# One 512 KB load cut into five copies, so that 9 of the 16 DMA engines carry more of it: linear ReLU attention on one Trainium2 core

## The chip, the core and the metric

The kernel runs on one core of a Trainium2 chip. The metric is the device time of one execution in microseconds (us), as the median of several runs. The profile comes from one more execution of the same program.

The core has five engines that matter here: TensorE (PE, matrix products), VectorE (DVE), ScalarE (ACT), GpSimd (POOL) and SyncE (SP). Data is moved between memory (HBM) and the core's own memory (SBUF) by 16 DMA engines that all copies share. A copy is issued by an engine's queue. In this kernel POOL issues most copies (the profile's queue q0) and SP issues the first four loads and the last three stores (queue q1). Each DMA engine serves both queues.

## What is computed

Q, K and V are float32, of shape batch 8, heads 12, sequence 512, depth 64. For each of the 96 heads:

```python
Q_feat = np.maximum(0, Q)
K_feat = np.maximum(0, K)
KV = np.einsum('bhkd,bhkv->bhdv', K_feat, V)
K_sum = np.sum(K_feat, axis=2)
numerator = np.einsum('bhqd,bhdv->bhqv', Q_feat, KV)
denominator = np.einsum('bhqd,bhd->bhq', Q_feat, K_sum)
return numerator / (denominator[:, :, :, None] + 1e-10)
```

## The kernel before, in words

The 96 heads are handled in 12 blocks `o` of 8 heads. A block has two groups `g = 2*o` and `g = 2*o + 1` of 4 heads each. In SBUF a group of K or V is a tile of 128 rows (partitions) of 16 x 64 = 1024 numbers, and a block of Q or of the output is 128 rows of 2048 numbers. In memory each row is one contiguous stretch: 4096 bytes for a group's row, 8192 bytes for a Q or output row.

**Loads.** The first two groups (block 0) are loaded as float32 by SP, in the loop of lines 111 to 115: K of group 0, V of group 0, K of group 1, V of group 1, each one copy of 128 x 4096 bytes into a tile `kv_first`. These tiles come from the pool `outp`, which later holds the output tiles `o_sb`. All other loads are issued by POOL and turned into bfloat16 on the way: `load_q(0)`, then `load(1)` to `load(5)`, each being K, V and Q of a block. From then on the order of POOL's queue is written out in `store` (line 262): the store of block `o`, then `load(o + 6)`. POOL's copies use eight semaphores in turn, so the ninth copy waits until the first has landed: at most eight are under way. The last two blocks are stored by SP (lines 267 and 270), the last one in two halves.

**Compute.** The order is written out by hand (`manual_schedule`), each engine running its instructions in program order. For a group, `prep` (line 144) has DVE build `kf` from K (line 147) and one half of `vo` from V (line 149), and `prep_v` (line 152) builds the other half of `vo`, on ACT (line 154) or DVE (line 156). `mm_kv` (line 159) multiplies them on PE into `ps_kv`, and `evac_kv` (line 167) copies the result to `kvd`. For a block, `qt` transposes Q on PE and applies the ReLU on ACT (line 190); `denom` (line 229) makes the reciprocal of the denominator; `out_t` (line 204) makes the numerators, transposed; `backs` (line 297) transposes them back on PE (line 250) and DVE multiplies them by the reciprocals into `o_sb` (line 256); `store` issues the copy to memory.

**The order around the change.** At the start DVE and ACT run `prep(0)`, `prep(1)` and, behind those, small set-up work of DVE (lines 284, 286, 140, 135, 137), then `mm_kv(0)`, `mm_kv(1)`, `qt(0)` and the loop over blocks of line 311. The V of group 1 is read by line 149 on DVE and line 154 on ACT. In DVE's queue the set-up work and `prep(2)` stand behind that instruction.

Of the kernel before, what the change touches and what calls it, by code (L numbers as in the profile page):

```python
# [10 lines left out]
def kernel(  # L11
# [7 lines left out]
    nc = tc.nc  # L19
    B, H, S, D = Q.shape  # L20
    assert D == 64
    P = 128
# [11 lines left out]
    DELAY = 5  # L34
    F32 = 2
    PAIRS = NO - 3

    fp32 = mybir.dt.float32
    bf16 = mybir.dt.bfloat16
# [19 lines left out]
    def view(X, f):  # L59
        return X.rearrange("b h s d -> (b h s d)").rearrange("(n p f) -> n p f", p=P, f=f)  # L60

    Qr, Kr, Vr, Or = view(Q, RQ * D), view(K, R * D), view(V, R * D), view(out, RQ * D)
# [27 lines left out]
    q_sb, k_sb, v_sb = {}, {}, {}  # L90

    def load_kv(o):
        pairs = [(kin.tile([P, 2, R * D], bf16, name="k_sb"), Kr, k_sb),
                 (vin.tile([P, 2, R * D], bf16, name="v_sb"), Vr, v_sb)]
        for t, _, sb in pairs:
            for i in range(2):
                sb[2 * o + i] = t[:, i].rearrange("p (r d) -> p r d", d=D)
        if o < PAIRS:
            for t, X, _ in pairs:
# [6 lines left out]
    def load_q(o):  # L106
        q_sb[o] = qin.tile([P, U, 2 * D], bf16, name="q_sb")
        nc.gpsimd.dma_start(out=q_sb[o].rearrange("p u f -> p (u f)"), in_=Qr[o], single_packet=True)  # L108


    for g in range(F32):
        kv = outp.tile([P, 2, R, D], fp32, name="kv_first", tag="o_sb")
        k_sb[g], v_sb[g] = kv[:, 0], kv[:, 1]
        nc.sync.dma_start(out=k_sb[g].rearrange("p r d -> p (r d)"), in_=Kr[g])
        nc.sync.dma_start(out=v_sb[g].rearrange("p r d -> p (r d)"), in_=Vr[g])
    load_q(0)
    make_identity(nc, ident)

# [210 lines left out]
    g = 2 * NO - 2  # L329
# [52 lines left out]
```

## Time and profile before

| what | us |
|---|---|
| median of 3 runs | 126.31 (125.97 to 126.70) |
| the profiled execution | 126.07 |
| its span in the profile | 124.3 |
| busy PE / DVE / ACT / POOL | 82.9 / 81.2 / 78.7 / 31.8 |
| V of group 1: issued by SP, landed | 2.12, 12.52 |
| first store (block 0): o_sb written, store issued by POOL | 28.39, 31.97 |
| last o_sb written; its store issued | 116.9; from 115.79 |

The span is the time from the first to the last instruction that the profiler recorded. The time of the execution is 1.8 us longer than the span. Times in the profile count from the span's start.

The profile can be read in several views: a page with busy shares, the span in 40 slices, DMA queues and the chain of waits; a timeline of each engine, where a bracket behind an instruction gives the idle time before it and what ended it; a table of windows with the DMA engines' busy share and GB/s. The trace also records every packet that a DMA engine moved: its start, its duration, its queue and its bytes. A row of a tile is one packet. Behind the last packet of a copy, each engine writes a 4-byte packet, which is how the copy reports that this engine's share is done.

The packet records do not name their DMA engine, but they can be sorted by engine: a packet begins a fixed few nanoseconds around the end of the one before it on the same engine (4 ns before it ends for a 4096-byte packet of q1, 19 ns for a packet of q0 that is turned into bfloat16), and each engine carries 8 rows of every 128-row copy and then the 4-byte packet. With these two rules the 10,256 data and 4-byte packets of both queues fall into 16 chains of equal content.

### The profile page before, as it was taken

The page shows a single profiled execution, that of the slowest core. Times are in us where ns is not written, and L with a number is a line of the kernel's source. Part 1 is how long each engine was busy: PE and PEld are TensorE (multiplying, and loading weights), DVE is VectorE, ACT ScalarE, POOL GpSimd, SP SyncE. Part 2 cuts the span into 40 slices and gives each one's busy share as a digit, 9 for nine tenths or more (in the row PEclk, how much of TensorE's full clock was granted, in tenths as well). Part 3 has the DMA queues.
Part 4 walks back from the last instruction along what each step waited for, and adds up shares of the span by engine and source line. Part 5 has one row for each costly group of instructions (what it writes and reads, how often), then busy time and mean ns, then how long its engine had stood idle before and what let it go on. Part 6 is the DMA issues. An engine that isn't in the chain of part 4 may idle for free.

```text
span 124.3 us, 2630 instructions
## 1 busy us (share of the span) xinstructions
PE 82.9 (67%) x1075; PEld 75.4 (61%) x1075; DVE 81.2 (65%) x176; ACT 78.7 (63%) x114; POOL 31.8 (26%) x56
## 2 busy tenths in 40 slices
PE   0041096997988898892890998697696595989100
PEld 0050095987978787791890798686685484979000
DVE  2614851979797997828825934969739639976600
ACT  0240639999897998974963657688389186456000
POOL 6932133222242123322231122143233221000000
PEclk9999999999999999999998559999999999999955
DMA  4999999999999999999999999999999999999992
GB/s 128 324 282 281 217 206 211 214 212 216 207 215 211 210 221 361 223 216 343 249 210 296 293 213 260 332 209 234 353 218 218 353 234 216 327 419 424 424 418 117
DMA packets 10268, 32.67 MB, mean 263 GB/s; under 512 B 912, under 2 KB 912, under 8 KB 8848
## 3 DMA queue, kind: packets, MB, share of 16 engines
q0 software_dynamic: 9248, 28.31, 95.0%
q1 hardware_dynamic: 1008, 4.19, 8.7%
q8 instruction: 8, 0.13, 0.4%
q14 instruction: 4, 0.03, 0.1%
HBM read 37.75 MB, written 12.58 MB: 405 GB/s over the span
## 4 chain that ended last, share of the span: by engine, by line
DMA 38%; DVE 29%; PE 17%; ACT 5%; issue 2%; SPq 1%; DVEq 1%; ACTq 0%; POOLq 0%
DMA v_sb<-in_V_dram 29%; DVE o_sb L256 13%; DMA kv_first<-in_V_dram 8%; PE ps_kv L161 8%; PE ps_bk L250 6%; DVE kf L147 4%; ACT qt L190 3%; DVE vo L149 3%; PE ps_qt L182 2%; ACT kvd L171 2%; DVE vo L156 2%; DVE den L240 2%; DVE own L235 1%; DVE rec L244 1%; DVEq L377 1%
## 5 line engine op out<-in xcount | busy, mean ns | idle before, releaser
L161 PE MATMUL ps_kv<-vo,kf 128*128 128x132 bf16 x384 | 29.2, 235 | 19.5 <-ACT vo L154 7.8
L161 PEld LDWEIGHTS <-kf 128*128 128x128 bf16 x384 | 26.3, 104 | 21.2 <-DVE vo L149 11.1
L256 DVE TENSOR_TENSOR o_sb<-ps_bk,rec 128x1024 f32<-128x1024 f32 x24 | 28.3, 1217 | 10.4 <-PE ps_bk L250 10.4
L171 ACT CAST kvd<-ps_kv 64x260 bf16<-64x260 f32 (+1 forms) x54 | 18.6, 345 | 15.6 <-PE ps_kv L161 13.4
L214 ACT COPY ot_sb<-ps_ot 128x1024 f32<-128x1024 f32 x22 | 21.9, 1014 | 5.5 <-PE ps_ot L212 5.0
L250 PE MATMUL ps_bk<-ident,ot_sb 128*128 128x128 f32 x192 | 23.0, 273 | 0.0
L147 DVE TENSOR_SCALAR kf<-k_sb,mask 128x1024 bf16<-128x1024 bf16 x44 | 18.5, 462 | 6.2 <-DMA k_sb<-in_K_dram 6.1
L190 ACT ACTIVATE qt<-ps_qt 128x1024 bf16<-128x1024 bf16 x23 | 22.4, 1030 | 0.1
L250 PEld LDWEIGHTS ps_bk<-ident,ot_sb 128*128 128x128 f32 x192 | 20.8, 141 | 0.0
L212 PE MATMUL ps_ot<-qt,kvd 128*128 128x256 bf16 x88 | 13.5, 283 | 9.6 <-DVE o_sb L256 9.5
L212 PEld LDWEIGHTS <-kvd 128*128 128x128 bf16 x88 | 8.5, 100 | 12.4 <-issue 11.4
L182 PE MATMUL ps_qt<-ident,q_sb 128*128 128x128 bf16 x192 | 14.4, 235 | 0.0
L149 DVE TENSOR_SCALAR vo<-v_sb,mask 128x1024 bf16<-128x1024 bf16 x22 | 10.6, 482 | 5.4 <-DMA v_sb<-in_V_dram 5.4
L154 ACT ACTIVATE vo<-v_sb,mask 128x1024 bf16<-128x1024 bf16 x10 | 11.5, 1153 | 3.2 <-DMA v_sb<-in_V_dram 3.1
L182 PEld LDWEIGHTS <-q_sb 128*128 128x128 bf16 x192 | 13.2, 106 | 0.3
L108 POOL DMA_DIRECT2D q_sb<-in_Q_dram x12 | 7.1, 590 | 18.0 <-DMA k_sb<-in_K_dram 9.9
L272 POOL DMA_DIRECT2D out_dram<-o_sb x10 | 5.7, 569 | 17.2 <-DVE o_sb L256 4.7
L232 PEld LDWEIGHTS <-qt 128*128 128x128 bf16 x192 | 6.7, 96 | 4.8 <-ACT qt L190 3.4
L232 PE MATMUL ps_den<-kvd,qt 128*128 128x16 bf16 x192 | 7.5, 179 | 2.7 <-ACT qt L190 2.1
L100 POOL DMA_DIRECT2D v_sb<-in_V_dram x8 | 5.8, 722 | 11.5 <-DMA q_sb<-in_Q_dram 5.7
L100 POOL DMA_DIRECT2D k_sb<-in_K_dram x8 | 5.9, 742 | 8.4 <-DMA v_sb<-in_V_dram 3.8
L235 DVE SCALAR_TENSOR_TENSOR own<-ps_den,mask_h 128x256 f32<-128x256 f32 x12 | 5.0, 415 | 3.3 <-PE ps_den L232 3.3
(30 smaller groups left out, 42.2 us busy)
## 6 DMA issues: line engine op xcount, KB each, us to landing
out_dram<-o_sb POOLq DMA_DIRECT2D x10, 1024.0 KB, 15.6
q_sb<-in_Q_dram POOLq DMA_DIRECT2D x12, 512.0 KB, 19.5
k_sb<-in_K_dram POOLq DMA_DIRECT2D x8, 512.0 KB, 19.9
v_sb<-in_V_dram POOLq DMA_DIRECT2D x8, 512.0 KB, 19.7
k_sb<-in_K_dram POOLq DMA_DIRECT2D x6, 256.0 KB, 13.3
v_sb<-in_V_dram POOLq DMA_DIRECT2D x6, 256.0 KB, 12.1
kv_first<-in_K_dram SPq DMA_DIRECT2D x2, 512.0 KB, 5.8
kv_first<-in_V_dram SPq DMA_DIRECT2D x2, 512.0 KB, 7.2
```

The costliest lines, as they stand in the source:

```text
L100: nc.gpsimd.dma_start(out=t, in_=X[2 * o:2 * o + 2].rearrange("g p f -> p g f"), single_packet=True)
L147: nc.vector.tensor_scalar(kf[g][:, :, s, :], k_sb[g], scalar1=0.0, scalar2=mask[:, 0, s:s + 1], op0=Alu.max, op1=Alu.mult)
L149: nc.vector.tensor_scalar(vo[g % NB][:, :, 0, 2:D + 2], v_sb[g], scalar1=mask[:, 1, 0:1], scalar2=None, op0=Alu.mult)
L161: nc.tensor.matmul(ps_kv[:, g % 2, 0:2 * (D + 2)].rearrange("p (t d) -> p t d", t=2), kf[g][:, r, :, :].rearrange("p s d -> p (s d)"), vo[ ...
L171: copy(kvd[o % NK][64 * c:64 * c + 64, 4 * gs.start + s:4 * gs.stop:2, c * D1:c * D1 + D1].rearrange("p (g t) d -> p g t d", t=2), ps_kv[6 ...
L182: nc.tensor.transpose(ps[:, u, :], q_sb[o][:, i * (U // 2) + u, :], ident)
L190: nc.scalar.activation(to, ps, Act.Relu)
L212: nc.tensor.matmul(ps[:, i], kvd[o % NK][:, h, 1:2 * D + 1], q[:, :, h, :], start=True, stop=True, skip_group_check=True)
L214: nc.scalar.copy(ot[o][:, :, 4 * j:4 * j + 4], ps.rearrange("p h u c -> p u h c"))
L232: nc.tensor.matmul(ps[:, u], qt_sb[o % NZ][:, u, :], kvd[o % NK][:, :, 0:2 * D1:2 * D1 - 1], start=True, stop=True, skip_group_check=True)
L250: nc.tensor.transpose(ps[:, 2 * v:2 * v + 2].rearrange("p c d -> p (c d)"), ot[o][:, 8 * j + v].rearrange("p h c -> p (h c)"), ident32)
L256: nc.vector.tensor_tensor(o_sb[:, rs], ps, rec[o][:, rs].unsqueeze(2).to_broadcast([P, 16, D]), op=Alu.mult)
```

## The change

V of group 1 is no longer one copy. Its first 672 columns are one copy of 128 rows of 2688 bytes. Its last 352 columns (1408 bytes a row) are four copies of 81, 27, 18 and 2 rows. A copy is split evenly over a number of DMA engines that divides its rows, at most 16: 81, 27 and 18 rows go to nine engines as 9, 3 and 2 rows each, and 2 rows go to two engines. So nine engines (carriers, below) move 14 tail rows each, two of them 15, and the other seven none. Nothing else is changed, except that line numbers behind the edit grow by 7.

```diff
+    VC = 672
...
-        nc.sync.dma_start(out=v_sb[g].rearrange("p r d -> p (r d)"), in_=Vr[g])
+        vf = v_sb[g].rearrange("p r d -> p (r d)")
+        if g == 0:
+            nc.sync.dma_start(out=vf, in_=Vr[g])
+            continue
+        nc.sync.dma_start(out=vf[:, 0:VC], in_=Vr[g][:, 0:VC])
+        for a, b in ((0, 81), (81, 108), (108, 126), (126, P)):
+            nc.sync.dma_start(out=vf[a:b, VC:], in_=Vr[g][a:b, VC:])
```

In the built program no engine's order of work changes but SP's, which has eight loads ahead of its three stores instead of four. The two readers of V of group 1 (line 149 on DVE, line 154 on ACT) wait on five semaphores instead of one. SP's copies have eight semaphores, which the eight loads now use up, so each of the three stores also waits for one of the first three loads.

## The prediction

> **What bounds the kernel now.** I read the DMA rows of the page first, because no computing engine is busy for more than 67% of the span.
>
> ```profile
> DMA  4999999999999999999999999999999999999992
> ...
> q0 software_dynamic: 9248, 28.31, 95.0%
> q1 hardware_dynamic: 1008, 4.19, 8.7%
> ```
>
> The 16 DMA engines are busy in every slice between the first and the last, and the two queues add up to over 100% (packets overlap a little). Next, the table of windows over the end; the last two columns are the DMA engines' share and GB/s.
>
> ```profile
> 114.00:116.00 2.00, 1.38 (x13) 1.14 (x11) 1.46 (x2) 0.03 (x1) 0.00 (x0) 1.00 1.02 430
> 116.00:118.00 2.00, 0.00 (x0) 0.00 (x0) 0.90 (x1) 0.00 (x0) 0.00 (x0) 1.00 1.01 426
> 118.00:120.00 2.00, 0.00 (x0) 0.00 (x0) 0.00 (x0) 0.00 (x0) 0.00 (x0) 0.66 1.00 420
> 120.00:122.00 2.00, 0.00 (x0) 0.00 (x0) 0.00 (x0) 0.00 (x0) 0.00 (x0) 0.50 0.87 350
> 122.00:124.00 2.00, 0.00 (x0) 0.00 (x0) 0.00 (x0) 0.00 (x0) 0.00 (x0) 0.50 0.18 74
> ```
>
> All computing ends at 116.9 us, and the DMA engines go on at full rate for some 4 us more, then fall off one after the other. So the end is set by the DMA engine that finishes last. Third, the chain of waits at its start, and DVE's timeline further on (the bracket is the idle time and what ended it):
>
> ```profile
> 2.12 10.40 DMA kv_first<-in_V_dram
> 12.52 0.03 issue
> 12.54 0.76 DVE vo L149
> ```
> ```profile
> 53.82 0.88 DVE L147 TENSOR_SCALAR kf<-k_sb,mask 128x1024 bf16<-128x1024 bf16 x2 [1.26 <-DMA k_sb<-in_K_dram]
> 56.34 0.49 DVE L149 TENSOR_SCALAR vo<-v_sb,mask 128x1024 bf16<-128x1024 bf16 x1 [1.64 <-DMA v_sb<-in_V_dram]
> 63.99 0.88 DVE L147 TENSOR_SCALAR kf<-k_sb,mask 128x1024 bf16<-128x1024 bf16 x2 [2.24 <-DMA k_sb<-in_K_dram]
> 66.54 0.49 DVE L149 TENSOR_SCALAR vo<-v_sb,mask 128x1024 bf16<-128x1024 bf16 x1 [1.66 <-DMA v_sb<-in_V_dram]
> ```
>
> The chain says that compute starts with the V that is changed here (landed at 12.52). DVE's timeline says that this start is not what sets the end: from 53.82 to 83.84 DVE waits eight times for loads, 11.5 us in all.
>
> **When each DMA engine finishes.** The packet records, sorted by engine, give the 4-byte packet that ends the last store:
>
> ```
> 7 engines: 121.16 121.25 121.42 121.55 121.61 121.64 121.64   (early)
> 2 engines: 122.20 122.24                                      (middle)
> 7 engines: 122.60 122.73 122.75 122.80 122.94 122.99 123.04   (late)
> ```
>
> All carry the same rows. Both middle engines and six of the seven late ones each moved one 16,384-byte packet of the queue "instruction" (892 to 975 ns), so they have more to do. Moving bytes from the late to the others would bring the end forward: the mean is 122.5.
>
> **Part 1: what the cut does to each engine's work.** While V of group 1 is moved, each engine alternates: one packet of q1, one of q0. The packets of one engine (start in ns, queue:bytes written):
>
> ```
> 9679 q0:2048   9832 q1:4096   10001 q0:2048   10154 q1:4096   10322 q0:2048
> ```
>
> A q0 packet takes 153 ns here, a 4096-byte q1 packet 168. The trace has no q1 packet between 4 and 4096 bytes. Bounds: bytes alone (26.6 B/ns, from 153.9 ns per 4096 bytes in unmixed stretches) below, 168 ns for every packet whatever its size above. I take 168 less the bytes saved, 115 ns for 2688 bytes and 67 ns for 1408, because unmixed packets read at 305 ns for 8192 bytes, 154 for 4096 and 6 for 4: time follows bytes with almost nothing on top.
>
> - Before, every engine: 8 x 168 = 1344 ns of q1.
> - Carrier: 8 x 115 + 14 x 67 + three more 4-byte packets of 3 = 1867 ns, 0.52 us more; for the two with a fifteenth tail row, 0.59 more.
> - The other seven: 8 x 115 = 920 ns, 0.42 us less.
>
> No engine idles between 3 and 121 us, so these shift the engines' ends one for one; the q0 packets in between are work that comes anyway.
>
> **Part 2: which engines these are** decides the sign, and packet records have no engine numbers. The late group is exactly seven, the gap from the other nine (122.24 to 122.60) is wider than any within it, and the shift between the two sets that the cut makes (0.94 to 1.01 us, by bytes alone 0.74) is near what would level them (123.04 - 122.24 = 0.80). I take the nine as early plus middle. Then the middle end at 122.76 to 122.83, the late at 122.62, the early below 122.3. The end moves from 123.04 to about 122.8: **0.24 us earlier**. By bytes alone it is 0.42; at 168 ns for every packet it is 1.5 later, the upper end of the unknown.
>
> The Trainium skill ("DMA: Bandwidth & Descriptors", How many engines (k)) says that a copy issued by SP takes the lowest-numbered k engines; which of my chains those are, no run here shows.
>
> **Part 3: V of group 1 lands later.** A carrier alternates its 22 data packets and 4 four-byte packets with as many q0 packets: 26 x 153 + 1867 = 5.85 us behind its end of K (8.61 to 9.49 by engine), against 2.73 before. That is 14.5 to 15.7, and the landing came 0.30 behind the last 4-byte packet: V lands at 14.8 to 16.0, I take 15.5, **3.0 us later**. SP issues four more copies at 0.43 us (rows of L115), until some 4.3 us, long before K is through; nothing else waits on SP until 112.
>
> Behind line 149 stand DVE's set-up work, `prep(2)` and, through `ps_kv` and `kvd`, everything of block 0, so all compute of the first blocks shifts by 3.0. Who waits? POOL's queue:
>
> ```profile
> 29.19 0.80 POOL L108 DMA_DIRECT2D q_sb<-in_Q_dram  x1 [2.72 <-DMA k_sb<-in_K_dram]
> 31.97 0.55 POOL L272 DMA_DIRECT2D out_dram<-o_sb  x1 [1.99 <-DVE kf L147]
> ...
> 41.84 0.55 POOL L272 DMA_DIRECT2D out_dram<-o_sb  x1 [2.16 <-DVE o_sb L256]
> ```
>
> Block 0's o_sb is written at 28.39, its store goes out at 31.97, paced by the landing of an earlier copy: 3.6 us of cover. Block 1: 35.47 against 41.84. A shift of 3.0 fits, and one up to 6 would delay POOL by 2.4, while POOL's copies land 20 us behind their issue: the engines would not run dry. DVE's waits at 53.82, 56.34 and 63.99 (5.1 us) then swallow the shift. Cost: 0. At the end, compute has some 4 us in hand (the last half store lands 7.6 us behind its issue).
>
> Five semaphores instead of one for V, and one more for each store, cost at most tens of ns off the path: 0.
>
> A rule of the Trainium skill speaks against the change: "Rules for kernel authors" on the same page wants all 16 engines used, and one 128-partition transfer instead of parts. By it this V lands later, as worked out above; this trace agrees that V is not what the end hangs on.
>
> **Sum.** 126.07 (profiled execution) - 0.24 = 125.83. The median of the runs is 0.24 above that execution, so 126.07 by the median; I predict 126.0.
>
> **Rivals.**
> - *Carriers include late engines.* At least two of any nine must be late or middle. If the worst is one of 122.60 to 123.04, the end is there plus 0.52 to 0.59: 123.12 to 123.63, so +0.1 to +0.6, 126.4 to 126.9. For it: nothing in the records ties chains to numbers. The same page of the Trainium skill ("Latency and other measured facts") says that engines 7 and 15 are usually slower; by that rule a carrier is late, with this result. Chance 0.27.
> - *Small packets cost more than their bytes*, nearer the 168 ns each: +0.4 to +1.5, 126.7 to 127.8. Against: the 4, 4096 and 8192 byte rows lie on one line. Chance 0.08.
> - *The late V costs all its delay* (slower): if block 0's start sets the end, as the chain's first 12 us suggest, +2.3 to +3.5, 128.6 to 129.8. It decides if the shift outlasts DVE's waits between 53 and 84 us (11.5 us), which it would have to exceed. Chance 0.04.
> - *The split is another one*: the tail rows fall on all 16 engines evenly. Then each gets about 0.1 to 0.2 more: 126.4. Chance 0.05.
> - *Bytes alone*, with the carriers I take: -0.42, 125.65 against the profiled execution, 125.9 by the median. Chance 0.11.
>
> Forecast: 0.45 (125.7 to 126.4). Range 125.4 to 127.1: it leaves out the late-V case and the upper half of the dear packets. About 0.5% (0.63 us) is what a measurement of this kernel can tell from no change. Faster by more than that (under 125.68): part of the last rival and an edge of the forecast, as single runs spread by 0.7 us, 0.15. Slower (over 126.94): late V, most of the dear packets and an edge of the first rival, 0.19. Between: 0.66.
>
> **What would show it.** Part 1: q1 packets of 2688 and 1408 bytes near 115 and 67 ns. Part 2: the last 4-byte packets of the 16 engines within 0.7 us or so of each other, besides the early ones, instead of 1.9. Part 3: V lands near 15.5, block 0's o_sb near 31.4, the store of block 0 unmoved near 32, DVE's first waits for loads gone. The prediction is wrong if the spread at the end grows, if DMA share falls below 0.99 before 120 us, or if DVE has no waits left by 84 us.

## The result and the profile after

The changed kernel takes 126.73 us (median of 7 runs, 126.58 to 127.11), the kernel before 126.01 us in the same measurement (7 runs, 125.96 to 126.7): a ratio of 1.0045, interval 1.0023 to 1.0067. It is slower by 0.45% by that ratio (the two medians lie 0.72 us apart). Predicted were 126.0 us and a gain of 0.24 us. The time lies within the range, but it moved the other way.

The profiled execution took 126.58 us with a span of 124.78, against 126.07 and 124.30 before. So 0.49 of the 0.51 us between these two are inside the span, and the two profiles can be compared.

First the page of the kernel after: the share of the DMA engines in 40 slices, and the two queues (packets, MB, share of 16 engines).

```profile
DMA  4999999999999999999999999999999999999991
...
q0 software_dynamic: 9248, 28.31, 94.6%
q1 hardware_dynamic: 1165, 4.19, 8.9%
```

Of the two, only q1's count of packets changed (1008 before, 1165 now: 157 more). The engines are still busy from the first slice to the last, so the end is again that of the last DMA engine. The table of windows over the end (PE, PEld, DVE, ACT, POOL, granted clock, DMA share, GB/s), after:

```profile
114.00:116.00 2.00, 1.91 (x22) 1.85 (x23) 1.21 (x4) 1.67 (x2) 0.00 (x0) 1.00 1.01 426
116.00:118.00 2.00, 1.12 (x11) 0.88 (x9) 1.72 (x2) 0.00 (x0) 0.00 (x0) 1.00 1.00 422
118.00:120.00 2.00, 0.00 (x0) 0.00 (x0) 0.64 (x1) 0.00 (x0) 0.00 (x0) 1.00 0.98 406
120.00:122.00 2.00, 0.00 (x0) 0.00 (x0) 0.00 (x0) 0.00 (x0) 0.00 (x0) 1.00 0.99 406
122.00:124.00 2.00, 0.00 (x0) 0.00 (x0) 0.00 (x0) 0.00 (x0) 0.00 (x0) 0.60 0.13 53
```

In the last two rows the DMA share was 0.87 and 0.18 before and is 0.99 and 0.13 now. The engines fall off closer together, as the cut was predicted to do. And yet the end is later: a share says nothing about the one engine that is last. Compute ends at 118.7 instead of 116.9 (DVE's 0.64 in the third row); whether that matters is the first question below.

The other rows that answer to the prediction: DVE's first use of V of group 1, POOL's store of block 0, and DVE's waits for loads from 53 to 84 us.

```profile
15.57 0.76 DVE L156 TENSOR_SCALAR vo<-kv_first,mask 128x1024 bf16<-128x1024 f32 x1 [4.40 <-DMA kv_first<-in_V_dram]
```
```profile
32.77 0.55 POOL L279 DMA_DIRECT2D out_dram<-o_sb  x1 [3.59 <-DVE o_sb L263]
```
```profile
63.90 0.88 DVE L154 TENSOR_SCALAR kf<-k_sb,mask 128x1024 bf16<-128x1024 bf16 x2 [0.38 <-DMA k_sb<-in_K_dram]
66.37 0.49 DVE L156 TENSOR_SCALAR vo<-v_sb,mask 128x1024 bf16<-128x1024 bf16 x1 [1.58 <-DMA v_sb<-in_V_dram]
```

V of group 1 is used from 15.57 on (12.54 before). The store of block 0 goes out at 32.77 (31.97 before) and now waits for DVE's o_sb: that was written 4.1 us later than before (32.47 against 28.39), not 3.0, which is more than the 3.6 us of cover. DVE's waits for loads at 53.82 and 56.34 are gone, and the first one left, at 63.90, has shrunk from 2.24 to 0.38 us: the delay is swallowed there.

**Where the 0.49 us of the span are.** Two things that neither the page nor the chain shows, but the records of packets and semaphores do. The first is the last 4-byte packet of each DMA engine (us). Each engine's packets can be strung together, since on one engine a packet starts where the one before it ended; the number and size of its q1 packets then tell whether it carries rows of the tail.

```
after, seven engines without tail rows:  121.27 122.13 122.13 122.28 122.29 122.43 122.46
after, nine engines with tail rows:      121.81 121.82 121.94 122.13 122.18 122.41 122.83 122.86 123.14
```

The last one moved from 123.04 to 123.14, and the landing of the last store from 123.374 to 123.570. The second is what SP does behind that landing. It passes its copies' semaphores one by one, then drains:

```
before  landing 123.374, passed 123.391, drain 123.456, end of span 124.297
after   landing 123.570, passed 123.587, five more waits passed at 123.649 123.708 123.769 123.829 123.890, drain 123.955, end of span 124.783
```

From landing to end are 0.92 us before and 1.21 after. The 0.49 us are 0.20 by the landing and 0.29 by this list.

### The profile page after: what moved, and what is told of

It reads as the page before. It is cut to its first block, busy times and chain, and to the rows that moved or that the text cites. A ratio compares the mean times of both kernels' runs of the same rounds, so it can differ in the third digit from the quotient of the medians.

```text
span 124.8 us, 2641 instructions
## 1 busy us (share of the span) xinstructions
PE 84.1 (67%) x1075; PEld 76.7 (61%) x1075; DVE 80.9 (65%) x176; ACT 79.1 (63%) x114; POOL 31.9 (26%) x56
## 3 DMA queue, kind: packets, MB, share of 16 engines
q1 hardware_dynamic: 1165, 4.19, 8.9%
## 4 chain that ended last, share of the span: by engine, by line
DMA 58%; DVE 17%; PE 15%; issue 2%; POOL 1%; DVEq 1%; ACT 0%; POOLq 0%
DMA v_sb<-in_V_dram 42%; DMA k_sb<-in_K_dram 16%; DVE o_sb L263 9%; PE ps_kv L168 6%; PE ps_bk L257 4%; PE ps_qt L189 3%; DVE kf L154 2%; DVE vo L156 1%; DVE vo L163 1%; DVEq L384 1%; PE ps_ot L219 1%; DVE den L247 1%; DVE rec L251 1%; DVE qt L195 1%; DVE own L242 1%
## 5 line engine op out<-in xcount | busy, mean ns | idle before, releaser
L168 PE MATMUL ps_kv<-vo,kf 128*128 128x132 bf16 x384 | 28.7, 234 | 22.3 <-ACT kvd L178 8.9
L168 PEld LDWEIGHTS <-kf 128*128 128x128 bf16 x384 | 25.8, 103 | 23.8 <-DVE vo L156 14.0
L219 PE MATMUL ps_ot<-qt,kvd 128*128 128x256 bf16 x88 | 14.4, 295 | 8.1 <-DVE o_sb L263 8.1
L189 PE MATMUL ps_qt<-ident,q_sb 128*128 128x128 bf16 x192 | 15.6, 246 | 0.0
L189 PEld LDWEIGHTS <-q_sb 128*128 128x128 bf16 x192 | 14.6, 114 | 0.4
L161 ACT ACTIVATE vo<-kv_first,mask 128x1024 bf16<-128x1024 f32 x2 | 2.3, 1153 | 7.7 <-DMA kv_first<-in_V_dram 7.7
```

The source lines that it names most:

```text
L161: nc.scalar.activation(vo[g % NB][:, :, 1, 2:D + 2], v_sb[g], Act.Copy, scale=mask[:, 1, 1:2])
L168: nc.tensor.matmul(ps_kv[:, g % 2, 0:2 * (D + 2)].rearrange("p (t d) -> p t d", t=2), kf[g][:, r, :, :].rearrange("p s d -> p (s d)"), vo[ ...
L189: nc.tensor.transpose(ps[:, u, :], q_sb[o][:, i * (U // 2) + u, :], ident)
L219: nc.tensor.matmul(ps[:, i], kvd[o % NK][:, h, 1:2 * D + 1], q[:, :, h, :], start=True, stop=True, skip_group_check=True)
```

## The theories and the experiments

- **Theory A (list of waits).** SP waits at the end for the semaphores of its copies in a fixed order. Before, with four loads, the last store's semaphore is the last of the list. With eight loads all eight semaphores are used, the stores take the first three again, and five waits stand behind the last store: about 5 x 0.06 = 0.30 us.
- **Theory B (late carrier).** One of the nine engines that carry the tail was late before, so what it was given comes out at the end. This is the first rival of the prediction.
- **Theory C (late compute).** V lands 3 us later, the last stores are issued later, and engines run dry.

**The list alone.** Into the kernel before, four tiny loads, which change nothing but the number of SP's loads (four, so eight loads):

```diff
+    scr = consts.tile([P, 4 * 16], fp32, name="scr")
+    for i in range(4):
+        nc.sync.dma_start(out=scr[0:2, 16 * i:16 * i + 16], in_=Kr[0][0:2, 16 * i:16 * i + 16])
     load_q(0)
```

> The kernel before, with V of group 1 whole, and four tiny loads (2 rows of 64 bytes each into a tile that nothing reads) behind SP's four loads, so that SP has eight loads ahead of its three stores, as in the changed kernel. Theory 1 (the list at the end): SP waits at the end for its copies' semaphores one after the other in a fixed order, about 61 ns each; with eight loads the last store's semaphore is third in the list and five more waits come behind it. Then the last packet ends as before, the last landing to the end of the span grows by 0.30 us, and the time is 126.3 against 126.0. Theory 2 (the DMA engines): only the unequal work of the DMA engines costs; then nothing moves here, 126.0.

126.29 against 126.09: ratio 1.0010, interval 0.9993 to 1.0026. In the profile, landing to end is 1.21 us, as in the changed kernel. With two such loads (range(2)) the list has seven waits behind the last store:

> The kernel before with two tiny loads behind SP's four: six loads, so the last store takes the first of the eight semaphores and seven waits stand behind it in the list. Theory of the list: 7 x 61 ns = 0.43 us more than before, 126.5, and in the profile 0.43 more between the last landing and the end of the span. Theory of the DMA engines alone: 126.1, no change.

126.34 against 126.20: 1.0023, interval 1.0006 to 1.0039; landing to end 1.34 us. Once more, on another chip:

> The kernel before with two tiny loads once more (seven waits behind the last store's). The first time it was 0.23% slower [0.06, 0.39], where the rows of the list say 0.43 us (0.34%). If the list costs its rows: 0.34% again. If something gives part of it back: 0.1 to 0.2%.

126.43 against 126.02: 1.0031, interval 1.0010 to 1.0052; landing to end 1.34 again. So in each profile the list is there to within 0.01 us, about 0.06 for each wait. In the times, each interval has room for it (0.30 us is 0.24%, 0.42 is 0.33%), but the middles are lower: 0.10, 0.23 and 0.31%. The list is real; that all of it reaches the time is not shown to better than about half.

**The list taken away.** The changed kernel with five tiny loads more, so that SP issues thirteen loads. They take the eight semaphores once and the first five again, and the three stores get the last three of the list:

```diff
+    scr = consts.tile([P, 5 * 16], fp32, name="scr")
+    for i in range(5):
+        nc.sync.dma_start(out=scr[0:2, 16 * i:16 * i + 16], in_=Kr[0][0:2, 16 * i:16 * i + 16])
```

> The changed kernel with five tiny loads (2 rows of 64 bytes) behind the cut V, so that SP has 13 loads and its three stores take the last three of the eight semaphores, as in the kernel before. Theory 1 (the list at the end): no wait stands behind the last store's, so 0.30 us of the loss comes back: 126.4, where the changed kernel has 126.73. Theory 2 (the DMA engines alone): no change against the changed kernel, 126.7.

126.54 against 126.09: 1.0042, interval 1.0024 to 1.0060. Landing to end is back at 0.91 us, but the last landing is at 123.985. So theory A alone falls: without the list, the change still costs time. The 126.4 that theory A expected did not come either: the ratio is that of the changed kernel (1.0045), so in the times nothing is seen to come back when the list goes (the intervals leave room for it).

**The cut without the carriers.** Two copies of 128 rows, so that all 16 engines carry the same; five loads, and the list is short:

```diff
+        nc.sync.dma_start(out=vf[:, 0:VC], in_=Vr[g][:, 0:VC])
+        nc.sync.dma_start(out=vf[:, VC:], in_=Vr[g][:, VC:])
```

> V of group 1 cut at column 672 as in the changed kernel, but the tail is one copy of 128 rows on all 16 engines: five loads of SP, so its stores hold the last three semaphores. Theory 1: only the cut's own cost is left, 8 x (116 + 69 - 168) = 0.14 us on every DMA engine: 126.1 to 126.2; V lands near 14.0. Theory 2 with the unequal carriers as the cause: the same 126.1 to 126.2. If instead the smaller packets, or the later V, cost what the changed kernel lost: 126.5 and more.

126.38 against 126.09: 1.0016, interval 0.9997 to 1.0034. That has room for the 0.14 us (0.11%) which the eight added packets cost each engine, by the times of Part 1 measured further down, and also for no cost. The same with three tiny loads, so that the list is that of the changed kernel:

> V of group 1 cut evenly at column 672 on all 16 engines (two copies of 128 rows), and three tiny loads (2 rows of 64 bytes into a tile that nothing reads), so that SP has eight loads and five waits stand behind the last store's in the list at the end. If the list costs what its rows say (0.30 us) and the even cut 0.14: 126.5 against 126.1 of the kernel before and 0.30 above the even cut with the short list. If the unequal work of the DMA engines is what costs: 126.2.

126.55 against 126.20: 1.0028, interval 1.0008 to 1.0048; landing to end 1.21. With the changed kernel once more in the same measurement:

> The changed kernel once more, on the same chip as the others of this call. List (0.30), more packets (0.12 on the mean) and nothing for the unequal work: 126.5. With the carriers among the late engines (0.5 for the unequal work): 126.9.

126.71 against 126.20: 1.0045, interval 1.0027 to 1.0063. And this profile answers theory C. SP's issues of the last stores in the profiles of the changed kernel, first and second:

```profile
117.53 1.47 SPq L274 DMA_DIRECT2D out_dram<-o_sb  x2
```
```profile
116.02 1.46 SPq L274 DMA_DIRECT2D out_dram<-o_sb  x2
```

Of the kernel before, in the second profile of it:

```profile
116.02 1.46 SPq L267 DMA_DIRECT2D out_dram<-o_sb  x2
```

The second profile of the changed kernel issues its last stores when the kernel before does, and its execution was no faster (126.72 us, the first 126.58). The first one's late compute went together with the granted clock. The PEclk rows of the first, the second and a third profile (told of below) of the changed kernel:

```profile
PEclk9999999999999999999999999599999769999996
```
```profile
PEclk9999999999999999999999999599999999999955
```
```profile
PEclk9999999999999999999999999589999859999996
```

All have 0.5 in the slice from 78 us; the first one has 0.7 and 0.6 besides, from 97 to 103 us, and the third 0.8 and 0.5. In the third the last stores go out at 118.09. That the clock is the cause was not tested. Theory C is out for this kernel: no DMA engine stood idle towards its last packet in the first or the second profile.

**More for the carriers.** The same rows of the tail, but 704 columns wide:

```diff
-    VC = 672
+    VC = 320
```

> The changed kernel with the cut at column 320 instead of 672: tail rows of 2816 bytes. With the rows of the changed kernel (116 ns for 2688 bytes, 69 for 1408, 168 for 4096, so 17 ns and 27.2 bytes a ns) a carrier has 0.87 us more than before (two of them 0.99), the other seven 0.83 less. Theory A, carriers are early and middle engines: the middle ends at 123.1 to 123.2, 0.1 to 0.2 behind before, and with the list 0.30: 126.5. Theory B, late engines are among the carriers: the last one ends 0.87 later, and with the list: 127.2.

127.44 against 126.20: 1.0099, interval 1.0073 to 1.0125. Theory B expected 127.2, theory A of this text 126.5. Its windows:

```profile
120.00:122.00 2.00, 0.00 (x0) 0.00 (x0) 0.00 (x0) 0.00 (x0) 0.00 (x0) 1.00 1.00 406
122.00:124.00 2.00, 0.00 (x0) 0.00 (x0) 0.00 (x0) 0.00 (x0) 0.00 (x0) 0.82 0.40 164
124.00:125.00 1.00, 0.00 (x0) 0.00 (x0) 0.00 (x0) 0.00 (x0) 0.00 (x0) 0.50 0.00 0
```

In the row from 122 to 124 the share is 0.40, where the changed kernel has 0.13: now the carriers hang behind, and the last landing is at 124.511.

**Whole rows instead of a cut.** V of group 1 as copies of whole rows, 80 on all engines and the rest on few, with six tiny loads (so no long list, and no packet under 4096 bytes but those of the tiny loads):

```diff
+        for a, b in ((0, P),) if g == 0 else ((0, 80), (80, 101), (101, 122), (122, 128)):
+            nc.sync.dma_start(out=vf[a:b], in_=Vr[g][a:b])
```

> V of group 1 cut by whole rows instead of columns (no small packets): copies of 80, 21, 21 and 6 rows, which 16, 7, 7 and 6 engines carry, so the seven lowest engines move 12 (one of them 11) rows and the other nine 5, where before each moved 8; six tiny loads put the stores last in the list at the end. Theory A: the changed kernel lost because two engines that also move instruction packets are among its nine carriers, and they are the two highest of the nine; then the seven have none. They end 0.67 later (121.2 to 121.7 become 121.9 to 122.4) and the others 0.50 earlier (123.04 becomes 122.5): 125.7 to 125.9, faster than before. Theory B: late engines are anywhere among the low numbers, or chance stalls set the end whatever the split: 126.2 to 126.8.

126.65 against 126.02: 1.0046, interval 1.0028 to 1.0065. With rows 80, 27, 18 and 3, that is to nine engines again, two rows more for each:

> The same with copies of 80, 27, 18 and 3 rows, which 16, 9, 9 and 3 engines carry: nine engines move 10 rows (three of them 11), the other seven 5; list and packets as in the run with seven. Theory A: the two carriers with instruction packets (122.80 and 122.94 before) end 0.34 later, at 123.1 to 123.3: 126.2 to 126.5, slower than the split over seven by 0.4 or more. Theory B: no difference between seven and nine beyond noise.

126.53 against 126.02: 1.0039, interval 1.0018 to 1.0059. The expectation that seven carriers would be faster than the kernel before (125.7 to 125.9), and faster than nine, failed. Neither the list nor small packets can be the reason for these two. What they share with the changed kernel is the uneven load. In the first of them SP's last store went out later still, and the share from 118 to 120 us is 0.94: some engines did run dry there, for half a microsecond to one, but they ended at 121.7 to 121.9 and the last one was none of them.

**Which engine is last.** To see it, both kernels were run once more for a further profile:

> The kernel before once more, unchanged, for a second profile of it. Theory (late engine): the engine with two 0.30 us holes and no instruction packet ends some tenths before the last one, as in the first profile (122.60 against 123.04), while the last ones carry instruction packets; the wait for the last store is the last of SP's waits, so landing to end is 0.92 us. Rival (the odd engine is level with the last one in a typical run, so that every tenth added to it costs a tenth): it ends within 0.15 us of the last. Time 126.0 to 126.2, ratio 1.000.

126.12 against 126.20: 0.9984, interval 0.9964 to 1.0003.

> The changed kernel a third time, for a third profile. Theory (late engine): the last 4-byte packet is on the engine with 0.30 us holes and no instruction packet, at 123.1 to 123.5, and the list of waits behind the last landing makes landing to end 1.21 us. Rival (the late compute end of the first profile sets it): DMA engines idle before 121 us. Time 126.7, ratio 1.0045 by both.

126.64 against 126.20: 1.0039, interval 1.0022 to 1.0056; landing to end 1.21. That makes 14 profiles. Besides q0 and q1, the pages list two more queues of the DMA engines, both called "instruction". In the page of the changed kernel:

```profile
q8 instruction: 8, 0.13, 0.4%
q14 instruction: 4, 0.03, 0.1%
```

In each profile eight engines moved one 16,384-byte packet of q8. The prediction counted these. The four packets of q14, of 8192 bytes each, it did not count. The last of the four starts between 117.5 and 121.4 us and takes 0.31 us of an engine that is still at work then. What comes next on that engine is slow: a 4096-byte packet takes 0.35 us instead of 0.155 and the one behind it 0.30, or an 8192-byte packet takes 0.65 to 0.66 instead of 0.31. Either way that is 0.35 us too long. Call it the odd engine. In the kernel before its packets run like this (start in ns, queue:bytes):

```
120551 q1:4096   120706 q14:8192   121012 q1:4   121018 q1:4096   121366 q1:4096   121666 q1:4096   121822 q1:4096
```

Without q14's rows the packet at 120706 looks like a hole of 0.30 us, and two expectations above call it that. In eleven of the 14 profiles the packets can be strung together so that it is clear which engine moved the first q14 packet, at 27.0 to 30.3 us: it is the odd engine again, with some 0.2 us of slow packets behind it. So the odd engine, too, moved 16,384 bytes of instruction. The two packets (0.63 us) and the slow ones behind them (0.55) are about what it ends behind the early engines in the kernel before, 1.0 to 1.4 us. The two other q14 packets, near 51 and near 90 us, are on two other engines. Where the odd engine ended (us), with the latest of the others beside it:

```
                                       odd engine   latest other
all engines alike: before                122.60        123.04
  before again                           122.41        123.26
  four tiny loads                        122.19        123.13
  two tiny loads, first and second       122.32 122.48 123.27 122.88
even cut, short and long list            122.87 122.65 123.47 123.29
changed: first, second, third            123.14 123.30 123.31   122.86 123.18 123.16
changed, stores last in list             123.56        123.14
column 320                               124.08        123.74
rows to seven / rows to nine             123.40 123.13 123.17 123.02
```

In all seven profiles with an even load an engine with a q8 packet is last and the odd one ends 0.4 to 0.95 us ahead of it. In all seven with an uneven load the odd one is last. In the six of these where the packets could be strung together over the whole run (all but rows to nine), it carries tail rows. So theory B holds. (In the rows-to-nine kernel its last half store could be followed only by its length, 1.25 us.) The table also answers the rival of the run "before again": the odd engine is not level with the last one before the change, it is some 0.7 us ahead, and passes it.

The size is only partly explained. The odd engine's mean over the five profiles of kernels with V whole is 122.40, over the three of the changed one 123.25: 0.85 later, where Part 1 gives 0.52. The slow packets behind the last q14 packet do not fill the gap, since they cost 0.35 on both sides. The remaining 0.33 is open. The other kernels show a rest as well: column 320 is 1.68 later where 0.87 was worked out, rows to seven 1.00 against 0.67, rows to nine 0.73 against 0.34. The mean end of all sixteen engines moves too, 122.26, 122.47 and 122.53 in the three profiles of the changed kernel, so single profiles do not settle tenths. One regular thing is on top: the landing comes 0.42 to 0.44 us behind the last 4-byte packet where the odd engine is last (0.41 in the rows-to-nine kernel), and 0.33 to 0.35 where another one is. That is 0.09 us more for the end.

## Why the prediction was wrong

Against its own profiled execution the prediction was 125.83, and 126.58 came: 0.75 us. The terms, from the profiles: the last packet at 123.14 instead of 122.80, 0.34; the landing behind it 0.43 instead of 0.34, 0.10; the list, 0.29; outside the span 0.02.

**The step that failed is in Part 2:** "I take the nine as early plus middle." Nothing in the records tied engines to carriers; the set was chosen because the gap between the groups looked like the shift that would level them. The right set was one engine away from it. The numbers fit the middle two of before being the two carriers with a q8 packet: with the shift they should end at 122.72 to 122.83, and the two such carriers ended at 122.83 and 122.86. They fit six of the seven late engines not being carriers: less 0.42 they should end at 122.18 to 122.62, and those with a q8 packet ended at 122.13 to 122.46. But the seventh late one, at 122.60, is the odd engine, and that one carries: 122.60 + 0.52 = 123.12, measured 123.14 in the first profile (that it fits so closely is luck, as the two later profiles have 123.30 and 123.31). The prediction had written that only six of the seven late engines moved an instruction packet. The seventh moved two, of the queue q14 on the same page. So the late group was made of two kinds, and the guess that all of it fell on one side had no ground. The sum that then follows is that of the first rival, +0.1, given 0.27. That rival gave 126.4 for +0.1; most of what is left to 126.73 is, by the profiles, the second step.

**The second step is in Part 3:** "Five semaphores instead of one for V, and one more for each store, cost at most tens of ns off the path: 0." A semaphore does cost tens of ns, 60, but on the path: behind the last landing there is nothing to hide it. Five of them are 0.29 us. No rival had it. The trace of before showed the order: its last semaphore passed 17 ns behind the landing, and the drain followed.

By the profiles either step alone would have taken away the forecast gain of 0.24. Without the list the change costs 1.0042 (1.0024 to 1.0060), so the list is not the whole. The even cut with the list costs 1.0028 (1.0008 to 1.0048): the uneven load is not needed for a loss, though part of this one is the even cut's own 0.14 us. These intervals overlap that of the changed kernel, so the times do not apportion the loss; the split of 0.29 and 0.20 is that of one pair of profiles.

The other steps:

- **Part 1 was right.** Packets of 2688 bytes follow each other on q1's turns at 116 ns and those of 1408 at 69 ns; 115 and 67 were predicted. The rival of dear small packets is out, and so is bytes alone (101 and 53 ns by 26.6 B/ns). A 4096-byte packet in unmixed stretches takes 155 ns in the trace, where the prediction read 153.9; nothing hangs on it.
- **Part 3's delay was right:** 15.5 was taken, DVE starts at 15.57. Block 0's o_sb was written at 32.47 instead of the 31.4 expected, so compute was 4.1 us late there and not 3.0, and its store went out 0.8 later rather than unmoved. DVE's waits swallowed it all the same. The rival that the late V costs all its delay (+2.3 to +3.5) is out.
- **The spread at the end** shrank as predicted: the standard deviation of the last packets of the sixteen engines is 0.66 us before and 0.44 after. Levelling most engines is worth nothing as long as one that was given more is last. The mean of the sixteen ends of before was written as 122.5; the prediction's table gives 122.16, so there was more room to level than was said, though no term of the sum hung on it.
- The Trainium skill ("DMA: Bandwidth & Descriptors", Latency and other measured facts) says that engines 7 and 15 are usually slower. By that rule a carrier is late, and the sign came out that way, but these traces give another reason: in the kernel before nine engines are late, eight with one packet of q8 and one with two of q14. Which numbers they have, no run here shows, so the result does not bear the rule out.

No version here beats the kernel before. A cut that spares the odd engine was not found: both ways of giving rows to few engines, nine or seven, reached it.

## What to carry to other kernels

Before load is moved between DMA engines, find for each late engine what makes it late, in every queue that the page lists and not only in those of the kernel's own copies. Then ask what ties an engine to the set that gets more: a match of sizes is no proof, and one wrong member turns the sign, because the end is a maximum and not a mean. Follow the last landing to the end of the span as well: SP passes its copies' semaphores one after the other, so adding loads at the start can put waits behind the last store at the end. Count copies so that the last store's semaphore stays last in that list.

## What the runs showed of the hardware that was not expected

- The list at the end costs 0.06 us for each wait behind the last store, and its length depends on the number of SP's copies: landing to end is 0.91 to 0.92 us with 4, 5 and 13 loads, 1.21 to 1.22 with 8, 1.34 with 6.
- An instruction packet of 16,384 bytes takes 0.88 to 0.98 us of one DMA engine, and q8 gave one to eight of the sixteen in every profile, at another time for each. With an even load these eight end about 1 us behind most of the rest.
- A second instruction queue, q14, gave four packets of 8192 bytes in every profile, near 27 to 30, 51, 90 and 117.5 to 121.4 us, 0.31 to 0.33 us each. The first and the last fall on one engine, and the packets behind them there are slow (some 0.2 and 0.35 us in all). Why those are slow was not tried.
- The granted clock falls in a second stretch in the first and third profile of the changed kernel and not in the second (PEclk rows above). SP's issue of the last stores came at 117.53 and 118.09 with it and at 116.02 without, and the time did not follow: 126.58 and 126.75 with, 126.72 without.
